# Conditioning rows one ahead, gate casts on VectorE, shorter conditioning stretches, and the modulated norm by pairs of blocks ahead of layer norms

## The chip, the cores and the metric

The kernel runs on one core of a Trainium2 chip. The metric is the device time of one execution in microseconds (us); below it stands as the median of three runs. All weights lie in HBM and are streamed once.

## What is computed

Two transformer nets in a row on 256 tokens of width 1024, two layers each, everything in float32. The first net has no conditioning; the second scales and shifts each normed input, and gates each branch, with vectors that are computed from one conditioning vector `c` (the six parts of `ada_w`). Cut to what matters here:

```python
for i in range(2):                                     # first net
    mix = concat(dsa_attention(...), spatial_gating(...)) @ w_o[i]
    x = layer_norm(ALPHA * x + mix, ln1_g[i], ln1_b[i])
    gate, up = split(x @ w_ffn_in[i], 2)
    x = layer_norm(ALPHA * x + (silu(gate) * up) @ w_ffn_out[i] + ple, ln2_g[i], ln2_b[i])

cond = silu(c)
for layer in range(2):                                 # second net
    sh1, sc1, g1, sh2, sc2, g2 = split(cond @ ada_w[layer] + ada_b[layer], 6)
    h = rms_norm(x, norm_mix[layer]) * (1 + sc1) + sh1
    x = x + g1 * (even_mixer(h) if layer == 0 else odd_mixer(h))
    h = rms_norm(x, norm_mlp[layer]) * (1 + sc2) + sh2
    a = relu(h @ mlp_w1[layer])
    x = x + g2 * ((a * a) @ mlp_w2[layer])
```

## The kernel before

**Products.** A float32 product is made as three products of parts: each weight unit (1024 columns of 128 rows, 512 KB) is split into a high part (`A.copy`, L417, on ScalarE) and the rest (`V.tensor_tensor` subtract, L418, on VectorE), each activation block likewise into `xh` and `xl`, and TensorE adds high by high, high by rest and rest by high (L446 to L448 for one half of the tokens; L467 to L469 and L482 to L484 where both halves are computed at once). The tokens are two halves of 128, `rr` = 0 and 1; their programs are generators that the main loop (from L1411 on) advances in turn, half 0 a little ahead.

**Order.** Weights come in one fixed order of units. `load` (L145) issues on SyncE's queue in program order into six buffers `w` (NW); the split goes into seven places `h`, `l` (NHI) and a few borrowed ones (`qTa`, `kTa`, `mix`). A list scheduler sets each engine's order; PRIORITY gives a group of instructions a head start in it, by so many places: `ln` 60 for layer norms, `mod` 15 for `modulated`, `ada` -15 for `conditioning`.

**Conditioning.** The generator `conditioning` (L663) goes through 12 jobs, first the shifts and scales of both layers, then the four gates. A job loads eight rows of `ada_w` (512 KB each, from the same six `w` buffers) and adds them up on VectorE (L673 for the first row, L675 for the other seven; in one buffer, `kTb`). A gate job then splits its sum as weights are split, the high part on ScalarE (L681), the rest on VectorE (L682), sums over the partitions with a matmul by ones (L686, L687) and adds the bias (L688). The main loop paces the steps of this generator: `conditioning_goal` spreads 45, 35 and 26 steps evenly over three stretches of units (`spans`, L1416): layer 0's feed-forward of the first net, layer 1's, and the first MLP of the second net, each up to where the next layer's input product begins. One more step comes after each of the last two stretches.

**Transitions.** `modulated` (L1040) makes the normed, scaled and shifted input of a mixer or MLP for one half. ScalarE squares x (L1047), GpSimd takes the power (L551), VectorE scales x by four blocks (L1053, into `hr`), TensorE transposes them (L1056). Then ScalarE applies scale and shift from PSUM, once for each of the four blocks into the high part `xh` and once again for each into `hid` in full float32 (L1061); VectorE subtracts `xh` from `hid` for all four together (L1063, 128x512), which gives `xl`. There are four such transitions: into the even mixer (about 640 to 653 us), into the first MLP (787 to 812), into the odd mixer (975 to 1002) and into the second MLP (1100 to 1130). Ahead of the first stands a layer norm (L560 to L568) of each half, ahead of the others the gated update of x (L1071, L1072). Just before the third the first MLP ends: its last hidden chunk goes through relu (L1029) and square (L1030) and is split by halves (L985, L986) before the last products, L446 to L448 on bank `a`. Into the odd mixer four tables of gains are also made (L292 to L295), from rows that are loaded into a `hid` buffer.

Of the kernel before, what the change touches and what calls it, by code (L numbers as in the profile page):

```python
# [14 lines left out]
AF = mybir.ActivationFunctionType  # L15
ALU = mybir.AluOpType
AX = mybir.AxisListType

P = 128
# [53 lines left out]

PRIORITY = {"mod": 15, "sb": 60, "sel": 30, "diff": 200, "ada": -15, "upd": 60, "fin": -15,
            "gelu": 400, "dil": 200, "rope": 400, "hd": -60, "sc": 60, "lat": -60, "ex": 30,
# [5 lines left out]
def body(ctx: ExitStack, tc: tile.TileContext, I, out):  # L81
# [51 lines left out]
    def r(ap):  # L133
        return ap.bitcast(F32R)
# [9 lines left out]
    def load(dst, src):  # L144
        ins = nc.sync.dma_start(dst, src)  # L145
        tc.keep_in_program_order(ins)
# [512 lines left out]

    COND_JOBS = [(l, j) for l in range(DEPTH) for j in (0, 1, 3, 4)] + [(0, 2), (0, 5), (1, 2), (1, 5)]  # L660
    COND_NAMES = ("sh1", "sc1", "g1", "sh2", "sc2", "g2")

    def conditioning():  # L663

        cond, ones, cols_a = C["cond"], C["ones"], C["cols_a"]
        for l, j in COND_JOBS:
            name = COND_NAMES[j]
            acc = new(act, [P, D], "kTb", 1)
            for k in range(KB):
                wt = new(ring, [P, UNIT], "w", NW)  # L670
                load(wt, I["ada_w_2"][l, k * P : (k + 1) * P, j * D : (j + 1) * D])
                if k == 0:
# [4 lines left out]
            if name[0] == "g":  # L677
                gt = new(act, [P, D], "par", 2)
                G.dma_start(gt, bcast(I["ada_b_2"][l : l + 1, j * D : (j + 1) * D], D))
                hi, lo = new(ring, [P, UNIT], "w", NW), new(ring, [P, UNIT], "w", NW)  # L680
                A.copy(r(hi), acc)  # L681
                V.tensor_tensor(r(lo), acc, hi, op=ALU.subtract)  # L682
# [357 lines left out]
    def modulated(l, rr, which):  # L1040
# [10 lines left out]
        for b0 in (0, 4):  # L1051
# [5 lines left out]
            full = new(act, [P, 512], f"hid{rr}", 2).rearrange("p (k n) -> p k n", k=4)  # L1057
            for dst in (r(hi[:, b0 : b0 + 4]), full):
                for j in range(4):
                    k = b0 + j  # L1060
                    A.activation(dst[:, j], ps[:, j * P : (j + 1) * P], AF.Identity, scale=sc[:, k : k + 1],  # L1061
                                 bias=sh[:, k : k + 1])
            V.tensor_tensor(r(lo[:, b0 : b0 + 4]), full, hi[:, b0 : b0 + 4], op=ALU.subtract)  # L1063
        return [(hi[:, k], lo[:, k]) for k in range(8)]
# [339 lines left out]
    def program(rr):  # L1404
        load_x(rr)
        for l in range(DEPTH):
# [8 lines left out]
    even, odd = first_unit["ein", 0], first_unit["oin", 0]  # L1415
    spans = [(first_unit["pg", 0, 0], first_unit["in", 1, 0]), (first_unit["pg", 1, 0], even),  # L1416
             (first_unit["w1", 0, 0], odd)]

# [86 lines left out]
```

## Time and profile before

| | |
|---|---|
| median of three runs | 1300.56 us (1298.23 to 1302.83) |
| the profiled execution | 1306.28 us |
| its span | 1304.6 us, that is 1.68 us lie outside the span |
| mean granted clock of TensorE | 0.991 |
| TensorE busy | 1269.1 us, 97% of the span |
| VectorE busy | 1030.9 us, 79% |
| ScalarE busy | 731.9 us, 56% |
| GpSimd busy | 47.1 us, 4% |
| the stretch 140 to 320 us (first feed-forward) | TensorE busy 180.00 of 180 us, DMA engines 87% |

The page is read from its shares to the stretches: TensorE's weight loads (PEld) run beside its matmuls, so the two shares do not add up. "idle before, releaser" in a row is how long the engine stood still ahead of an instruction and whose end let it go. The granted clock in a row by stretch is a share of full speed: 1.00 is 2.4 GHz, 0.50 is 1.2 GHz.

### The profile page before, as it was taken

To read this page: it belongs to the slowest core of one execution; us is meant where nothing else is said; L and a number is where in the kernel's file an instruction comes from. 1 tells how busy PE (TensorE), PEld (TensorE's weight loads), DVE (VectorE), ACT (ScalarE), POOL (GpSimd) and SP (SyncE) were. 2 spreads that over 40 slices of the span, in tenths; PEclk is the share of its full clock that TensorE was granted. 3 is DMA by queue.
4 is the path that set the end of the run, shared out by engine and by line. 5 is a ranking of instruction groups with operands and counts; after the bars stand their busy time and mean duration, and the time that the engine had idled before them with its cause. 6 is when DMAs were issued, how large, how long until landed. Compare 5 with 4: busy or idle time off the path is not lost.

```text
span 1304.6 us, 21751 instructions
## 1 busy us (share of the span) xinstructions
PE 1269.1 (97%) x7894; PEld 1130.3 (87%) x7894; DVE 1030.9 (79%) x2142; ACT 731.9 (56%) x1500; POOL 47.1 (4%) x109
## 2 busy tenths in 40 slices
PE   7999999999999999999899998999989999999998
PEld 6887999998888899999798986989877888799997
DVE  6979998987988999877779868776577997865552
ACT  5655445543565455444577767554447776854551
POOL 2010000000000000000110000000001000000000
PEclk9999999999999999999899999999989999999999
DMA  8545888995654689887454435776765635566631
GB/s 274 191 159 160 298 313 301 335 340 169 182 193 156 200 304 336 285 262 246 159 157 137 139 122 178 245 258 223 243 209 134 194 96 163 172 204 192 190 115 49
DMA packets 121804, 270.08 MB, mean 207 GB/s; under 512 B 9587, under 2 KB 30160, under 8 KB 121696
## 3 DMA queue, kind: packets, MB, share of 16 engines
q1 hardware_dynamic: 120304, 265.62, 62.2%
q0 software_dynamic: 1392, 3.07, 1.1%
q8 instruction: 62, 1.02, 0.3%
q14 instruction: 46, 0.38, 0.1%
HBM read 267.60 MB, written 1.05 MB: 206 GB/s over the span
## 4 chain that ended last, share of the span: by engine, by line
PE 80%; DVE 9%; DMA 4%; ACT 3%; issue 2%; POOL 1%; SPq 0%; POOLq 0%; DVEq 0%; ACTq 0%
PE m L469 10%; PE m L467 10%; PE m L468 10%; PE m L446 7%; PE m L448 7%; PE m L447 7%; PE a L482 5%; PE a L483 5%; PE a L484 5%; PE a L610 2%; DVE l L418 2%; PE a L446 2%; PE a L448 2%; PE a L447 2%; DMA w<-in_ada_w 1%
## 5 line engine op out<-in xcount | busy, mean ns | idle before, releaser
L417 ACT CAST h<-w 128x512 fp32r<-128x512 f32 (+3 forms) x634 | 354.2, 605 | 233.2 <-PE m L448 45.9
L418 DVE TENSOR_TENSOR l<-w,h 128x512 fp32r<-128x512 f32 (+3 forms) x634 | 399.5, 662 | 48.1 <-ACT h L417 47.2
L467 PE MATMUL m<-xh,h 128*128 128x256 f32 x832 | 232.5, 279 | 0.0
L468 PE MATMUL m<-xl,h 128*128 128x256 f32 x832 | 232.0, 279 | 0.0
L469 PE MATMUL m<-xh,l 128*128 128x256 f32 x832 | 232.0, 279 | 0.0
L446 PE MATMUL m<-h,xh 128*128 128x512 f32 (+3 forms) x544 | 208.2, 384 | 3.7 <-ACT h L417 3.0
L448 PE MATMUL m<-h,xl 128*128 128x512 f32 (+3 forms) x544 | 206.2, 381 | 4.4 <-DVE xl L1063 4.4
L447 PE MATMUL m<-l,xh 128*128 128x512 f32 (+3 forms) x544 | 206.0, 380 | 0.6 <-DVE l L418 0.4
L467 PEld LDWEIGHTS m<-xh,h 128*128 128x128 f32 x832 | 156.4, 188 | 0.4
L468 PEld LDWEIGHTS m<-xl,h 128*128 128x128 f32 x832 | 156.4, 188 | 0.3
L469 PEld LDWEIGHTS m<-xh,l 128*128 128x128 f32 x832 | 156.3, 188 | 0.2
L675 DVE SCALAR_TENSOR_TENSOR kTb<-w,cond,kTb 128x1024 f32<-128x1024 f32 x84 | 107.5, 1279 | 49.8 <-DMA w<-in_ada_w 49.3
L448 PEld LDWEIGHTS m<-h,xl 128*128 128x128 f32 x544 | 103.9, 191 | 18.2 <-DVE xl L1063 5.3
L446 PEld LDWEIGHTS m<-h,xh 128*128 128x128 f32 x544 | 104.2, 192 | 16.8 <-ACT h L417 3.8
L447 PEld LDWEIGHTS m<-l,xh 128*128 128x128 f32 x544 | 103.9, 191 | 13.8 <-DVE l L418 1.8
L482 PE MATMUL a<-h,hh 128*128 128x512 f32 x216 | 84.4, 391 | 0.0
L483 PE MATMUL a<-l,hh 128*128 128x512 f32 x216 | 84.4, 391 | 0.0
L484 PE MATMUL a<-h,hl 128*128 128x512 f32 x216 | 84.3, 390 | 0.0
L992 ACT CAST hh<-hid 128x512 fp32r<-128x512 f32 x44 | 27.3, 622 | 55.9 <-PE a L483 41.8
L417 ACT CAST qTa<-w 128x512 fp32r<-128x512 f32 x60 | 34.4, 622 | 34.0 <-DMA w<-in_w_ffn_in 12.8
L417 ACT CAST kTa<-w 128x512 fp32r<-128x512 f32 x60 | 34.8, 626 | 29.3 <-PE m L469 7.8
L484 PEld LDWEIGHTS a<-h,hl 128*128 128x128 f32 x216 | 40.7, 188 | 8.6
(455 smaller groups left out, 2469.9 us busy)
## 6 DMA issues: line engine op xcount, KB each, us to landing
w<-in_mlp_w SPq DMA_DIRECT2D x128, 512.0 KB, 4.3
w<-in_ada_w SPq DMA_DIRECT2D x96, 512.0 KB, 5.0
w<-in_w_ffn_in SPq DMA_DIRECT2D x80, 512.0 KB, 5.0
w<-in_w_ffn_out SPq DMA_DIRECT2D x44, 512.0 KB, 5.4
w<-in_odd_w_in SPq DMA_DIRECT2D x24, 512.0 KB, 4.4
w<-in_even_w_in SPq DMA_DIRECT2D x24, 384.0 KB, 3.6
w<-in_w_in SPq DMA_DIRECT2D x16, 512.0 KB, 5.5
w<-in_w_o SPq DMA_DIRECT2D x16, 512.0 KB, 5.7
```

Of the source, the lines that this page charges most:

```text
L417: split = [A.copy(r(ht[:, c]), wt[:, c]), V.tensor_tensor(r(lt[:, c]), wt[:, c], ht[:, c], op=ALU.subtract)]
L418: V.tensor_tensor(r(lt[:, c]), wt[:, c], ht[:, c], op=ALU.subtract)]
L446: T.matmul(ps, r(xh), r(wh[:, cols]), start=first, stop=False)
L447: T.matmul(ps, r(xh), r(wl[:, cols]), start=False, stop=False)
L448: mm = T.matmul(ps, r(xl), r(wh[:, cols]), start=False, stop=last)
L467: T.matmul(ps, r(wh[:, cols]), r(XH[:, :, k]), start=first, stop=False)
L468: T.matmul(ps, r(wh[:, cols]), r(XL[:, :, k]), start=False, stop=False)
L469: T.matmul(ps, r(wl[:, cols]), r(XH[:, :, k]), start=False, stop=last)
L482: T.matmul(ps, r(xh), r(wh[:, cols]), start=start and k == 0, stop=False)
L483: T.matmul(ps, r(xh), r(wl[:, cols]), start=False, stop=False)
L484: T.matmul(ps, r(xl), r(wh[:, cols]), start=False, stop=False)
L675: V.scalar_tensor_tensor(acc, wt, cond[:, k : k + 1], acc, op0=ALU.mult, op1=ALU.add)
```

## The change

Four things are changed.

1. `conditioning` issues the load of each `ada_w` row one step ahead of the step that adds it. It does not do so across two places (COND_PAUSES): the first row of jobs 5 and 9 is loaded in its own step.
2. The high part of a gate's sum is cast on VectorE (`V.tensor_copy`) instead of on ScalarE (`A.copy`).
3. The second and third stretch of conditioning begin later and end earlier: the second has 60 units instead of 74 for its 35 steps, the third 52 instead of 64 for its 26.
4. `modulated` has priority 100 instead of 15, and works by pairs of blocks: two activations into `hid`, a ScalarE cast of the pair into `xh` (128x256), a VectorE subtract of the pair into `xl`. The second set of activations is gone.

```diff
-PRIORITY = {"mod": 15, "sb": 60, "sel": 30, "diff": 200, "ada": -15, "upd": 60, "fin": -15,
+PRIORITY = {"mod": 100, "sb": 60, "sel": 30, "diff": 200, "ada": -15, "upd": 60, "fin": -15,
...
+    COND_PAUSES = (5, 9)
...
-        for l, j in COND_JOBS:
+        ahead = []
+
+        def fetch_row(job, k):
+            l, j = COND_JOBS[job]
+            ahead.append(new(ring, [P, UNIT], "w", NW))
+            load(ahead[-1], I["ada_w_2"][l, k * P : (k + 1) * P, j * D : (j + 1) * D])
+
+        for job, (l, j) in enumerate(COND_JOBS):
             name = COND_NAMES[j]
             acc = new(act, [P, D], "kTb", 1)
             for k in range(KB):
-                wt = new(ring, [P, UNIT], "w", NW)
-                load(wt, I["ada_w_2"][l, k * P : (k + 1) * P, j * D : (j + 1) * D])
+
+                if not ahead:
+                    fetch_row(job, k)
+                if k < KB - 1:
+                    fetch_row(job, k + 1)
+                elif job + 1 < len(COND_JOBS) and job + 1 not in COND_PAUSES:
+                    fetch_row(job + 1, 0)
+                wt = ahead.pop(0)
...
-                A.copy(r(hi), acc)
+                V.tensor_copy(r(hi), acc)
                 V.tensor_tensor(r(lo), acc, hi, op=ALU.subtract)
...
-            for dst in (r(hi[:, b0 : b0 + 4]), full):
-                for j in range(4):
+            for j0 in (0, 2):
+                pair, two = slice(b0 + j0, b0 + j0 + 2), full[:, j0 : j0 + 2]
+                for j in (j0, j0 + 1):
                     k = b0 + j
-                    A.activation(dst[:, j], ps[:, j * P : (j + 1) * P], AF.Identity, scale=sc[:, k : k + 1],
+                    A.activation(full[:, j], ps[:, j * P : (j + 1) * P], AF.Identity, scale=sc[:, k : k + 1],
                                  bias=sh[:, k : k + 1])
-            V.tensor_tensor(r(lo[:, b0 : b0 + 4]), full, hi[:, b0 : b0 + 4], op=ALU.subtract)
+                A.copy(r(hi[:, pair]), two)
+                V.tensor_tensor(r(lo[:, pair]), two, hi[:, pair], op=ALU.subtract)
...
-    spans = [(first_unit["pg", 0, 0], first_unit["in", 1, 0]), (first_unit["pg", 1, 0], even),
-             (first_unit["w1", 0, 0], odd)]
+    spans = [(first_unit["pg", 0, 0], first_unit["in", 1, 0]),
+             (first_unit["gate", 1, 0], first_unit["down", 1, 4]),
+             (first_unit["w1", 0, 1], first_unit["w2", 0, 6])]
```

Three places show how instructions move. The names are a buffer's tag and its running number; a digit before the first underscore, as in `hid0`, is the half. In the changed file the lines lie further down: L688 and L690 are the old L673 and L675, L1063 the old L1048, L1068 the old L1053, L1071 the old L1056, L1080 the old L1063.

VectorE at the transition into the even mixer, before: half 1's layer norm (L560 to L568) and half 0's first two `xl` (L1063).

```order
L560 BN_STATS ln_st_1235_7323<-x1_149 128x6
L418 TENSOR_TENSOR l_1259_7438<-w_1257_7436,h_1258_7437 128x336
L562 BN_AGGR ln_mv_1236_7326<-ln_st_1235_7323 128x2
L418 TENSOR_TENSOR l_1263_7466<-w_1261_7464,h_1262_7465 128x384
L563 TENSOR_SCALAR ln_mv_1236_7326<-ln_mv_1236_7326 128x1
L567 SCALAR_TENSOR_TENSOR x1_149<-x1_149,ln_mv_1236_7326,par_1186_7082 128x512 x2
L568 SCALAR_TENSOR_TENSOR x1_149<-x1_149,pw_y_1237_7329,par_1187_7084 128x512 x2
L1063 TENSOR_TENSOR xl_78<-hid0_1218_7238,xh_77 128x512
```

The same place after:

```order
L560 BN_STATS ln_st_1235_7321<-x1_149 128x6
L1080 TENSOR_TENSOR xl_78<-hid0_1218_7238,xh_77 128x256
L562 BN_AGGR ln_mv_1236_7324<-ln_st_1235_7321 128x2
L418 TENSOR_TENSOR l_1259_7434<-w_1257_7432,h_1258_7433 128x336
L1080 TENSOR_TENSOR xl_78<-hid0_1218_7238,xh_77 128x256
L563 TENSOR_SCALAR ln_mv_1236_7324<-ln_mv_1236_7324 128x1
L567 SCALAR_TENSOR_TENSOR x1_149<-x1_149,ln_mv_1236_7324,par_1189_7091 128x512
L1080 TENSOR_TENSOR xl_78<-hid0_1221_7254,xh_77 128x256
L568 SCALAR_TENSOR_TENSOR x1_149<-x1_149,pw_y_1237_7327,par_1190_7093 128x512
L1080 TENSOR_TENSOR xl_78<-hid0_1221_7254,xh_77 128x256
```

Half 0's `xl` moved from behind half 1's whole layer norm to between its first steps.

TensorE at the transition into the first MLP, before: half 0's transposes (L1056), its first products (bank `m0_1642`), and half 1's mixer output product (banks `m1_1673` and `m1_1678`, of which some rows are left out).

```order
L1056 MATMUL a0_1638_9088<-ident_70,hr0_1637_9086 128x128 x3
L446 MATMUL m0_1642_9105<-qTa0_1627_9045,xh_77 128x512
L447 MATMUL m0_1642_9105<-qTa1_1628_9046,xh_77 128x512
L1056 MATMUL a0_1638_9088<-ident_70,hr0_1637_9086 128x128
L446 MATMUL m1_1673_9230<-kTa_1585_8886,xh_77 128x512
L447 MATMUL m1_1673_9230<-kTa_1585_8886,xh_77 128x512
L448 MATMUL m1_1673_9230<-kTa_1585_8886,xl_78 128x512
...
L446 MATMUL m1_1678_9254<-h_1622_9027,xh_77 128x512
...
L448 MATMUL m0_1642_9105<-qTa0_1627_9045,xl_78 128x512
```

The same place after:

```order
L1071 MATMUL a0_1638_9083<-ident_70,hr0_1637_9081 128x128 x4
L446 MATMUL m0_1642_9099<-qTa0_1627_9041,xh_77 128x512
L447 MATMUL m0_1642_9099<-qTa1_1628_9042,xh_77 128x512
L448 MATMUL m0_1642_9099<-qTa0_1627_9041,xl_78 128x512
...
L446 MATMUL m0_1642_9099<-h_1644_9101,xh_77 128x512
...
L446 MATMUL m1_1673_9224<-kTa_1585_8882,xh_77 128x512
```

Before, twelve products of half 1 stand between half 0's first product and the first that reads `xl`; after, eighteen products of half 0 come in a row, three for each of six blocks, and half 1's follow.

ScalarE at the end of the first MLP, before: splits of the next weights (L417), the gate's cast (L681), relu (L1029) and the split by halves (L985).

```order
L417 CAST mix0_1958_11011<-w_1957_11010 128x512 x2
L681 CAST w_2005_11229<-kTb_1896_10649 128x1024
L417 CAST h_1963_11031<-w_1962_11030 128x512 x2
L417 CAST h_1966_11045<-w_1965_11044 128x512 x2
L1029 ACTIVATE hid0_1935_10917<-m0_1920_10784 128x512
L417 CAST h_1999_11194<-w_1998_11193 128x512
L1029 ACTIVATE hid1_1936_10920<-m1_1921_10785 128x512
L985 CAST hr0_1937_10923<-hid0_1935_10917 128x256
```

The same place after (L1044 is the old L1029, L1000 the old L985):

```order
L417 CAST mix0_1960_11009<-w_1959_11008 128x512 x2
L417 CAST h_1964_11026<-w_1963_11025 128x512 x2
L417 CAST h_1967_11040<-w_1966_11039 128x512 x2
L1044 ACTIVATE hid0_1939_10921<-m0_1924_10787 128x512
L417 CAST h_1999_11184<-w_1998_11183 128x512
L1044 ACTIVATE hid1_1940_10924<-m1_1925_10788 128x512
L1000 CAST hr0_1941_10927<-hid0_1939_10921 128x256
```

The gate's cast is gone from ScalarE's row; on VectorE it now stands 16 rows behind the last row sum (L690) of its job.

## Rows read from the trace of the kernel before

**Rows 1.** Section 1 of the page: busy time, share of the span and instructions.
```profile
PE 1269.1 (97%) x7894; PEld 1130.3 (87%) x7894; DVE 1030.9 (79%) x2142; ACT 731.9 (56%) x1500; POOL 47.1 (4%) x109
```

**Rows 2.** By stretch: length, then busy PE, PEld, DVE, ACT, POOL; PEclk, DMA share, GB/s.
```profile
140.00:320.00 180.00, 180.00 (x1310) 170.12 (x1309) 159.72 (x237) 84.89 (x154) 0.00 (x0) 1.00 0.87 301
460.00:600.00 140.00, 140.00 (x1066) 134.32 (x1065) 117.67 (x177) 69.62 (x125) 0.00 (x0) 1.00 0.88 302
786.00:812.00 26.00, 22.23 (x113) 17.38 (x112) 21.12 (x37) 20.64 (x54) 2.62 (x3) 0.93 0.62 198
1100.00:1130.00 30.00, 28.20 (x138) 21.65 (x138) 22.69 (x42) 23.12 (x57) 1.86 (x2) 1.00 0.38 122
...
643.80:650.30 6.50, 4.58 (x17) 4.43 (x18) 5.32 (x10) 3.18 (x11) 1.67 (x3) 0.50 0.91 324
970.40:974.70 4.30, 4.28 (x10) 3.04 (x11) 2.67 (x7) 1.47 (x4) 0.00 (x0) 0.50 0.80 236
999.00:1002.10 3.10, 2.91 (x11) 2.72 (x12) 3.10 (x7) 1.76 (x6) 0.00 (x0) 0.50 0.54 205
```

**Rows 3.** Timeline of PE behind three transitions: start, duration, instruction [idle before, releaser].
```profile
645.72 0.65 PE L448 MATMUL m<-h,xl 128*128 128x336 f32 x1 [4.44 <-DVE xl L1063]
...
970.42 0.80 PE L446 MATMUL a<-qTa,hr 128*128 128x512 f32 x1 [4.53 <-ACT hr L985]
...
999.19 1.97 PE L1056 MATMUL a<-ident,hr 128*128 128x128 f32 x8 [2.46 <-DVE hr L1053]
```

**Rows 4.** Timeline of ACT, half 0 into the even mixer.
```profile
639.54 1.50 ACT L1061 ACTIVATE xh<-a,mod0sh,mod0sc 128x128 fp32r<-128x128 f32 x4
640.93 1.51 ACT L1061 ACTIVATE hid<-a,mod0sh,mod0sc 128x128 f32<-128x128 f32 x4
```

**Rows 5.** Timeline of DVE, the same place.
```profile
640.71 0.69 DVE L560 BATCH_NORM_STATS2 ln_st<-x 128x6 f32<-128x512 f32 x1
...
642.33 1.40 DVE L567 SCALAR_TENSOR_TENSOR x<-x,ln_mv,par 128x512 f32<-128x512 f32 x2
643.65 1.41 DVE L568 SCALAR_TENSOR_TENSOR x<-x,pw_y,par 128x512 f32<-128x512 f32 x2
644.98 0.68 DVE L1063 TENSOR_TENSOR xl<-hid,xh 128x512 fp32r<-128x512 f32 x1
```

**Rows 6.** Timeline of ACT, end of the first MLP, then (last two rows) of the second.
```profile
964.46 1.05 ACT L681 CAST w<-kTb 128x1024 fp32r<-128x1024 f32 x1 [6.40 <-DVE kTb L675]
965.42 2.17 ACT L417 CAST h<-w 128x512 fp32r<-128x512 f32 x4
...
969.96 0.71 ACT L985 CAST hr<-hid 128x256 fp32r<-128x256 f32 x2 [0.88 <-DVE hid L1030]
...
1277.29 1.30 ACT L1029 ACTIVATE hid<-m 128x512 f32<-128x512 f32 x2 [6.67 <-PE m L469]
1278.65 1.42 ACT L985 CAST hr<-hid 128x256 fp32r<-128x256 f32 x4
```

**Rows 7.** Timeline of DVE into the first MLP (first row) and the odd mixer.
```profile
795.41 1.28 DVE L675 SCALAR_TENSOR_TENSOR kTb<-w,cond,kTb 128x1024 f32<-128x1024 f32 x1
...
996.84 0.22 DVE L292 TENSOR_TENSOR rope_ck<-turns,hid 128x64 f32<-128x64 f32 x1 [0.77 <-DMA hid<-in_moba_k_norm]
...
997.38 0.21 DVE L1048 TENSOR_SCALAR rms_s<-rms_s 128x1 f32<-128x1 f32 x1
```

**Rows 8.** Groups by line and shape: busy, mean ns of one, idle before and releasers.
```profile
L675 DVE SCALAR_TENSOR_TENSOR kTb<-w,cond,kTb 128x1024 f32<-128x1024 f32 x84 | 107.5, 1279 | 49.8 <-DMA w<-in_ada_w 49.3 <-DVE kTa L418 0.3
L673 DVE TENSOR_SCALAR kTb<-w,cond 128x1024 f32<-128x1024 f32 x12 | 9.0, 749 | 9.2 <-DMA w<-in_ada_w 9.2
...
L986 DVE TENSOR_TENSOR hr<-hid,hr 128x256 fp32r<-128x256 f32 x12 | 4.4, 418 | 0.0
```

**Rows 9.** Waits of SyncE's queue from 140 to 320: us in total, times, longest.
```profile
SPq L145 <- DVE l L418: 70.7, 44, 15.1
SPq L145 <- DVE kTb L675: 31.6, 26, 3.3
```

## The prediction

> **What bounds the kernel now.** I read the page's busy times first, then the time by stretch, then the waits. TensorE is busy for 1269.1 of the span's 1304.6 us [rows 1], so 35.5 us is all that can come back without less arithmetic. Nothing is to be had in the long feed-forward stretches: TensorE is busy 180.00 of 180 us and 140.00 of 140 there, at granted clock 1.00 [rows 2]. VectorE's 49.3 us of waiting for conditioning rows [rows 8] costs nothing by itself as long as TensorE has split weights in stock. What is lost stands at the start, at the end, and where one layer hands over to the next. At those places two things are paid: TensorE's idle time, and then the time in which its clock is granted at 0.50 (1.2 GHz) after the pause, in which busy time is worth half. I call the places T1 (into the even mixer), T2 (into the first MLP), T3 (end of the first MLP), T4 (into the odd mixer) and T5 (into the second MLP). At stake are:
> - T1: 4.44 idle [rows 3], and half of 4.58 busy at 0.50 [rows 2], 2.29: 6.7.
> - T2: 26.00 less 22.23 not busy, 3.8, and 0.07 of the clock over 22.23, 1.6 [rows 2]: 5.3.
> - T3: 4.53 idle [rows 3], and half of 4.28 [rows 2], 2.1: 6.6 (rounded down).
> - T4: 2.46 idle [rows 3], and half of 2.91 [rows 2], 1.5: 3.9.
> - T5: 30.00 less 28.20, 1.8, at full clock [rows 2].
>
> Together 24.3 us; the change touches all five places.
>
> **The change part by part. T3: the cast leaves ScalarE.** The chain here reads backwards. TensorE stands for 4.53 us until the last hidden chunk is split by halves (L985 on ScalarE) [rows 3]. Ahead of L985 on ScalarE stands relu, ahead of that four weight splits of 2.17 us together, and ahead of those the gate's cast L681, which began at 964.46 after 6.40 us in which ScalarE waited for VectorE's last conditioning row [rows 6]. ScalarE takes its instructions in order, so everything queued behind L681 stood with it. After the change the cast is on VectorE, behind the sum that it needs anyway, and the third stretch ends early enough that the last sum is made 16 VectorE instructions ahead of it. What is late next is then relu itself, behind TensorE's own product. The second MLP, which has no conditioning beside it, shows that form: relu waits for TensorE only, and L985 follows directly [rows 6]; TensorE has other products of the same bank to run meanwhile. So I take the whole 6.6; the lower bound is 5, if L985 still waits 0.88 for the square as it does now [rows 6] and TensorE pays that and some clock. Each of the four casts now takes VectorE between 0.75 (one fp32 source, 128x1024) and 1.28 (two sources) [rows 8], 3 to 5 us in all. That is covered: VectorE waits 49.3 us for conditioning rows [rows 8] that now land a step ahead. If this cover were gone, a cast would delay one weight split by about its own length.
>
> **T1: pairs ahead of the layer norm.** Half 0's `hid` is complete at 640.93 + 1.51 = 642.44 [rows 4], but its `xl` starts only at 644.98, behind half 1's layer norm, 1.40 and 1.41 [rows 5]. After the change the first `xl` stands behind L560 alone. ScalarE then needs two activations and a cast of 256 for a pair: 2 x 0.35 (1.39 between two groups of four [rows 4]) + 0.35 (half of 0.71 [rows 6]) = 1.05, so the first pair is ready at about 640.7. VectorE is in L560 from 640.71 for 0.69 [rows 5], then takes 0.42 for the subtract [rows 8]: TensorE starts at about 641.8 instead of 645.72, 3.9 us earlier, and with idle of half a microsecond left the clock's 2.3 should stay too. From this 6.2 I take off two things. TensorE needs six matmuls for a pair, at full clock 6 x 0.135 (half of 4.58 / 17 [rows 2]) = 0.8, while ScalarE delivers one in 1.05, over three further pairs 0.7 to 1: I take 0.9. And half 1's layer norm now waits behind four subtracts, 4 x 0.42 = 1.7 less the overlap with work that it has to wait for anyway: 1.0, which half 1's own products show unless half 0's cover it. That leaves 4.3; bounds 2.5 (nothing of the clock comes back, and half 1 pays half of the 1.0: 3.9 - 0.9 - 0.5) and 6.2.
>
> **T4: the odd mixer.** Half 1's L1053 waits for the mean square, L1048 at 997.38, which stands behind gain tables whose rows wait for DMA (0.77 at the last) [rows 7]. The order after still has these tables ahead of it. But they load into a `hid` buffer that half 0 gives back, and half 0 is done earlier by its new place. I take half of the 3.9, 2.0; bounds 0 and 3.9.
>
> **T2: the first MLP.** Before, twelve products of half 1 lie between half 0's first product and the first that reads `xl`; after, half 0's come in a row. So TensorE meets the wait for `xl` uncovered. On VectorE two weight splits and one conditioning row of 1.28 [rows 7] still stand between the scaling and the first subtract: 2 x 0.65 + 1.28 + 0.42 = 3.0, against the eight transposes (1.97 at half clock [rows 3], so 1.0) that TensorE runs meanwhile: about 2.0 to 2.2 idle here. Of the 3.8 not busy now no single row gives a split; I put a third, 1.2, at this point. Half 1's products later cover its own norm better than now. Net loss 1.0; bounds from 4 lost (the whole wait shown, and the clock with it) to 2 gained.
>
> **T5** has the same new order without conditioning rows in between: 0, from -1 to +1.
>
> **Stretches and rows ahead.** 35 steps in 60 units instead of 74 and 26 in 52 instead of 64 are no denser than the first stretch's 45 in 74, during which TensorE never stood [rows 2]. Their price is taken as nothing, with the second rival below as its bound.
>
> **More instructions.** 16 subtracts of 512 become 32 of 256, each pair 2 x 0.418 - 0.688 = 0.15 us dearer [rows 5, 8], 2.4 us of VectorE in all, on the path only at T1, where it is in the 0.42. ScalarE loses half of its activations and gains 16 casts; it becomes freer.
> The Trainium skill, VectorE: DVE Perf Modes, section on the TRN2 errata, speaks against this part: a fixed cost per instruction is paid again by every small tile, so tiles of 512 elements or more are to be preferred. By that rule the pairs would be a loss of 2.4 us and the sum 9.5 instead of 11.9; the rows agree on the price of a piece, and say that here a wait of 2.5 us is taken away with it.
>
> **The sum.** 6.6 + 4.3 + 2.0 - 1.0 + 0 = 11.9 us. The profiled execution is 1306.28, 5.7 above the median; its span of 1304.6 would become 1292.7. Against the median: 1300.56 - 11.9 = 1288.7.
>
> **The rivals.**
> - It doesn't do all that it says: conditioning rows still stand at T2, and what half 0 gains at T1 half 1 gives back. Then T3 6.6, T1 2.5, T2 -4, T4 0, T5 -1: 4.1 gained, 1296.5. For it speaks the order of VectorE at T2, against it that half 0's products cover half 1's norm.
> - The row ahead takes a `w` buffer. In the conditioning stretches one more of six buffers is held by a row that waits its turn. SyncE's queue waits there 70.7 + 31.6 = 102.3 us of 180 for a buffer [rows 9]; with five serving where six did, this grows by a fifth, 20.5, and by the same share 15.9 in the 140 us of the second stretch, 36.4 in all. The stock of split units takes a part: at most seven places of 180 / 74 = 2.4 us each, 17 per stretch. With half of it standing, 36.4 - 17 = 19.4 comes through: 1308.1. It decides as soon as TensorE's stock runs out in a stretch; against it is that TensorE shows not one pause there now, with DMA at 0.87 [rows 2].
> - Everything comes back: T1 6.2, T3 6.6, T4 3.9, T2 2: 18.7, 1281.9.
> - The pairs are dearer than the wait that they save (the 2.4 us all on the path): 1291.1.
>
> **How the numbers follow.** Chances: the forecast 0.57, dearer pairs 0.05, everything back 0.10, half done 0.20, the held buffer 0.08. A measurement of this kernel can tell 0.3%, 3.9 us, from no change: faster is below 1296.7, slower above 1304.5. The half-done case sits on that bound, so half of its 0.20 is "same": faster 0.57 + 0.05 + 0.10 + 0.10 = 0.82, same 0.10, slower 0.08. The range goes from 1282 (everything back) to 1299, the half-done case with the runs' own 2.3 above their median; left out are the held buffer, half of everything back and a little of the half-done case, 0.18.
>
> **What the changed profile would show.** T3: no pause over 1 us ahead of the products that read `hr`, and ScalarE's relu released by TensorE. T1: the first L448 near 641.8, the pause under 1 us, clock 1.00 behind it, and a new short pause ahead of half 1's products. T2: one pause of about 2 us ahead of the first L448 on `m0`, released by the pair's subtract. T4: the tables' DMA wait gone or shorter. VectorE's wait for conditioning rows well under 49 us. I am wrong if TensorE pauses in 140 to 320 or 460 to 600, or if the pauses at T1 and T3 merely move to half 1.

## The result, and the profile after

The changed kernel is slower: 1310.65 us median of six runs (1307.40 to 1312.00) against 1299.33 (1298.09 to 1302.83) of the kernel before; the ratio is 1.0077, 95% interval 1.0053 to 1.0100. The prediction was 1288.7, with a range of 1282 to 1299. The profiled execution took 1311.92 us, its span is 1310.2.

Section 1 of its page, beside [rows 1]:

```profile
PE 1267.7 (97%) x7894; PEld 1128.9 (86%) x7894; DVE 1035.5 (79%) x2162; ACT 718.8 (55%) x1464; POOL 46.6 (4%) x109
```

and the one row of its section 5 in which something new stands (busy, mean ns of one, idle before and its releaser):

```profile
L467 PE MATMUL m<-xh,h 128*128 128x256 f32 x832 | 233.1, 280 | 9.6 <-DVE mod1sc L718 9.5
```

TensorE has the same work and 97% again. But L467, the first product of a feed-forward unit, now waits 9.5 us, and for an addition of the conditioning. In the kernel before it never waited, as the same group of its instructions shows:

```profile
L467 PE MATMUL m<-xh,h 128*128 128x256 f32 x832 | 232.5, 279 | 0.0
```

The stretches of the changed kernel, in the columns of [rows 2], place it:

```profile
140.00:320.00 180.00, 179.85 (x1309) 169.94 (x1309) 160.34 (x238) 88.21 (x159) 0.00 (x0) 1.00 0.87 306
460.00:580.00 120.00, 120.00 (x895) 114.31 (x894) 105.59 (x153) 60.25 (x108) 0.00 (x0) 1.00 0.89 307
592.00:602.00 10.00, 1.40 (x6) 1.43 (x7) 7.05 (x14) 1.62 (x3) 0.00 (x0) 0.56 0.85 282
786.00:812.00 26.00, 21.65 (x125) 17.63 (x124) 17.63 (x39) 15.18 (x38) 1.47 (x1) 0.93 0.47 143
1100.00:1130.00 30.00, 29.78 (x157) 24.05 (x156) 24.52 (x48) 18.90 (x43) 0.55 (x1) 1.00 0.41 132
```

The feed-forward stretches are as full as before up to 580. Between 592 and 602 TensorE is busy 1.40 of 10 us. TensorE's timeline there, and at the transitions (start, duration, instruction, idle before and releaser):

```profile
589.20 0.31 PE L713 MATMUL m<-ada_q,quarters 128*128 128x32 f32 x2
...
590.83 0.28 PE L469 MATMUL m<-xh,l 128*128 128x256 f32 x1
600.60 0.55 PE L467 MATMUL m<-xh,h 128*128 128x256 f32 x1 [9.50 <-DVE mod1sc L718]
...
653.71 0.42 PE L446 MATMUL m<-h,xh 128*128 128x336 f32 x1 [0.87 <-ACT xh L1079]
657.87 0.42 PE L448 MATMUL m<-h,xl 128*128 128x336 f32 x1 [0.34 <-DVE xl L1080]
...
691.17 0.62 PE L446 MATMUL m<-h,xh 128*128 128x384 f32 x2 [1.50 <-ACT h L417]
...
805.69 0.50 PE L446 MATMUL m<-qTa,xh 128*128 128x512 f32 x1 [0.89 <-ACT xh L1079]
807.73 0.50 PE L448 MATMUL m<-qTa,xl 128*128 128x512 f32 x1 [1.31 <-DVE xl L1080]
...
1004.63 0.55 PE L1071 MATMUL a<-ident,hr 128*128 128x128 f32 x3 [0.89 <-DVE hr L1068]
```

and VectorE's in the pause:

```profile
593.38 1.28 DVE L690 SCALAR_TENSOR_TENSOR kTb<-w,cond,kTb 128x1024 f32<-128x1024 f32 x1 [3.41 <-DMA w<-in_ada_w]
594.58 2.49 DVE L418 TENSOR_TENSOR l<-w,h 128x512 fp32r<-128x512 f32 x4
...
598.57 1.28 DVE L690 SCALAR_TENSOR_TENSOR kTb<-w,cond,kTb 128x1024 f32<-128x1024 f32 x1 [1.50 <-DMA w<-in_ada_w]
599.78 0.68 DVE L718 TENSOR_TENSOR mod1sc<-m,cols_a 32x8 f32<-32x8 f32 x4
```

Read together: a shift or scale job ends with a small matmul (L713) into one of the two `m` banks of half 0, at 589.20. The next feed-forward product needs that bank. It comes free when VectorE reads it (L718). But VectorE takes its instructions in order, and ahead of L718 stand rows of the next job (L690), and these wait for DMA, 3.41 and 1.50 us. So TensorE, with nothing amiss in its weights, stood until 600.60.

Two executions can be lined up by the share of TensorE's matmul columns done. Done so for the changed kernel (1311.92) against a second trace of the kernel before (1297.93, the first experiment below):

| stretch of the second trace, us | what lies there | forecast, us | measured, us |
|---|---|---|---|
| to 583 | start, both first layers | 0 | +0.8 |
| 583 to 608 | the new pause | 0 | +11.1 |
| 633 to 784 | T1 (to 660) and the even mixer | -4.3 | -4.8, then +2.3 |
| 784 to 834 | T2 | +1.0 | +5.0 |
| 960 to 985 | T3 | -6.6 | -0.2 |
| 985 to 1035 | T4 | -2.0 | +0.1 |
| 1035 to 1135 | T5 | 0 | -0.3 |
| sum | | -11.9 | +14.0 |

### The profile page after: what moved, and what is told of

Its sections match the earlier page's. It is cut to its first block, busy times and chain, and to the rows that moved or that the text cites. A ratio compares the mean times of both kernels' runs of the same rounds, so it can differ in the third digit from the quotient of the medians.

```text
span 1310.2 us, 21731 instructions
## 1 busy us (share of the span) xinstructions
PE 1267.7 (97%) x7894; PEld 1128.9 (86%) x7894; DVE 1035.5 (79%) x2162; ACT 718.8 (55%) x1464; POOL 46.6 (4%) x109
## 5 line engine op out<-in xcount | busy, mean ns | idle before, releaser
L417 ACT CAST h<-w 128x512 fp32r<-128x512 f32 (+3 forms) x634 | 354.9, 604 | 260.2 <-PE m L468 51.9
L467 PE MATMUL m<-xh,h 128*128 128x256 f32 x832 | 233.1, 280 | 9.6 <-DVE mod1sc L718 9.5
L446 PE MATMUL m<-h,xh 128*128 128x512 f32 (+3 forms) x544 | 208.6, 384 | 6.3 <-ACT h L417 3.7
L448 PE MATMUL m<-h,xl 128*128 128x512 f32 (+3 forms) x544 | 206.0, 381 | 0.6 <-DVE xl L1080 0.6
L467 PEld LDWEIGHTS m<-xh,h 128*128 128x128 f32 x832 | 157.1, 189 | 10.4 <-issue 10.0
L690 DVE SCALAR_TENSOR_TENSOR kTb<-w,cond,kTb 128x1024 f32<-128x1024 f32 x84 | 107.7, 1282 | 52.7 <-DMA w<-in_ada_w 52.6
L446 PEld LDWEIGHTS m<-h,xh 128*128 128x128 f32 x544 | 104.1, 192 | 20.7 <-ACT h L417 4.4
L448 PEld LDWEIGHTS m<-h,xl 128*128 128x128 f32 x544 | 104.0, 191 | 14.0 <-DVE xl L1080 1.1
L417 ACT CAST kTa<-w 128x512 fp32r<-128x512 f32 x60 | 34.5, 619 | 34.9 <-PE m L469 7.7
L417 ACT CAST qTa<-w 128x512 fp32r<-128x512 f32 x60 | 34.9, 623 | 28.8 <-PE a L484 9.4
L417 ACT CAST mix<-w 128x512 fp32r<-128x512 f32 x60 | 34.6, 620 | 25.0 <-PE m L468 10.5
```

The costliest lines, as they stand in the source:

```text
L417: split = [A.copy(r(ht[:, c]), wt[:, c]), V.tensor_tensor(r(lt[:, c]), wt[:, c], ht[:, c], op=ALU.subtract)]
L446: T.matmul(ps, r(xh), r(wh[:, cols]), start=first, stop=False)
L448: mm = T.matmul(ps, r(xl), r(wh[:, cols]), start=False, stop=last)
L467: T.matmul(ps, r(wh[:, cols]), r(XH[:, :, k]), start=first, stop=False)
L690: V.scalar_tensor_tensor(acc, wt, cond[:, k : k + 1], acc, op0=ALU.mult, op1=ALU.add)
```

## The experiments

The times are medians of ten or twelve runs, where nothing else is said, each beside the median of the kernel before that was measured with it. The ratio and its 95% interval in brackets are an estimate of their own and differ a little from the quotient of the two medians.

**Was the first trace a common one?** The kernel before, unchanged.

> The kernel before, unchanged, for a second trace. The prediction took its terms from one execution of 1306.28 us, 7 us above the median of 1299.3. If that execution was a common one with a slow start, the idle ahead of the four transitions is as before (4.4, 3.8, 4.5, 2.5 us). If it lost more at the transitions than most executions do, the pauses here are shorter by some 5 to 7 us in all, and the gains of the forecast were too large by as much.

It took 1297.93 us, a single run. T1 was as before (4.45 idle), T4 1.91. T3 was not. ScalarE and TensorE at the end of the first MLP in this second trace:

```profile
959.30 1.05 ACT L681 CAST w<-kTb 128x1024 fp32r<-128x1024 f32 x1 [6.70 <-DVE kTb L675]
...
964.80 0.71 ACT L985 CAST hr<-hid 128x256 fp32r<-128x256 f32 x2 [0.86 <-DVE hid L1030]
...
966.36 0.50 PE L448 MATMUL a<-qTa,hr 128*128 128x512 f32 x1 [0.37 <-DVE hr L986]
```

The chain is that of [rows 6], the same cast behind the same row with even more waiting, and 5.5 us from the cast to the split by halves in both. But VectorE added the last row 5.2 us earlier. Most of that comes from three of the rows before it, for which it waited 1.48, 3.58 and 2.97 us here and 2.76, 4.48 and 4.51 in the first trace. TensorE was at the place at the same time in both (965.9 and 966.0), so it paused 0.37 us instead of 4.53. The term of 6.6 is the price of one execution.

**Reading the bank earlier**, on the changed kernel.

```diff
+                with tc.high_priority(400):
+                    ps = bank("m", 0)
+                    T.matmul(ps[:, 0:32], C["quarters"], part, start=True, stop=True)
...
+                    for q in range(4):
+                        at_q = slice(32 * q, 32 * q + 32)
+                        V.tensor_tensor(m[at_q], ps[at_q, q:32:4], bcol[at_q], op=ALU.add)
```

> The changed kernel; only the last step of a shift or scale job (the matmul by quarters and the four bias additions that empty its bank) gets a head start of 400 places, so that VectorE reads the bank ahead of more of the next job's rows. Theory A (TensorE stood 9.5 us at 591 us because the bank of the up product was still held by this job, whose reader stood behind the next job's rows on VectorE): the pause goes, 1299 to 1301. Theory B (the row ahead starves the weights): the pause stays or only changes its name, 1308 to 1312.

1304.39 us against 1301.24 (ratio 1.0025, 1.0007 to 1.0044): neither forecast. The pause near 590 is gone, as the stretch shows (columns of [rows 2]):

```profile
580.00:610.00 30.00, 30.00 (x228) 28.73 (x227) 23.82 (x40) 14.17 (x25) 0.00 (x0) 1.00 0.86 293
```

But the earlier matmul has to wait for its own bank, and TensorE in order with it, 0.61 to 1.12 us in three places. One of them in TensorE's timeline:

```profile
494.91 0.41 PE L714 MATMUL m<-ada_q,quarters 128*128 128x32 f32 x2 [1.01 <-DVE hid L1028]
```

In this execution T2 also cost 7.6 us, with the clock at 0.50 for some 13 us.

**The old stretches**, on the changed kernel.

```diff
-             (first_unit["gate", 1, 0], first_unit["down", 1, 4]),
-             (first_unit["w1", 0, 1], first_unit["w2", 0, 6])]
+             (first_unit["pg", 1, 0], even),
+             (first_unit["w1", 0, 0], odd)]
```

> The changed kernel with the three conditioning stretches of before; rows ahead, casts and pairs stay. Theory A: the last job of the second stretch ends behind the up product again, with 80 products instead of 14 between its matmul and the next product that needs the bank; no pause near 591, but the conditioning is near the transitions again: 1298 to 1303. Theory B: the row ahead still takes a buffer, 1306 to 1311.

1300.11 against 1301.24 (0.9985, 0.9967 to 1.0003): theory A. No pause near 590.

**No rows ahead**, on the changed kernel.

```diff
-                if not ahead:
-                    fetch_row(job, k)
-                if k < KB - 1:
-                    fetch_row(job, k + 1)
-                elif job + 1 < len(COND_JOBS) and job + 1 not in COND_PAUSES:
-                    fetch_row(job + 1, 0)
+                fetch_row(job, k)
                 wt = ahead.pop(0)
```

> The changed kernel, but every conditioning row is loaded in the step that adds it, as before; stretches, casts and pairs stay. Theory A: the place of the job's end between gate and up product is the same, seven rows instead of eight stand ahead of the reader, so a pause of 4 to 10 us stays near 591: 1304 to 1311. Theory B: the pause goes with the held buffer, 1297 to 1300.

1305.04 against 1301.24 (1.0017, 1.0002 to 1.0032): theory A. The pause stays at its place, half as long in this execution (with the clock behind it 7.5 us are lost there instead of 11.1), and by the two ratios the kernel is 0.6% faster than the changed one. TensorE's timeline:

```profile
593.52 0.55 PE L467 MATMUL m<-xh,h 128*128 128x256 f32 x1 [4.81 <-DVE mod1sc L713]
```

**The casts alone**, on the kernel before.

```diff
-                A.copy(r(hi), acc)
+                V.tensor_copy(r(hi), acc)
```

> The kernel before, with the cast of the gates on VectorE and nothing else. In the second trace of the kernel before the pause at the end of the first MLP was 0.37 us instead of 4.53: the execution that the prediction read was one of those in which a late conditioning row holds ScalarE. Theory C (a pause that comes in some executions, taken away by this part alone): the slow end of the spread goes, the median falls by 1.5 to 3 us against the kernel before of the same call, and no pause over 1 us at that place. Rival (the late row holds something else as well, VectorE's splits for one): median within 1 us of the kernel before, the pause comes back under another releaser.

1302.32 against 1300.20 (1.0010, 0.9994 to 1.0027), runs from 1297.51 to 1305.98. Theory C fell: the pause at T3 was 0.37 in this trace, but the spread is as wide as that of the kernel before. It does not come from T3 alone; in this execution T2 and T4 ran partly at clock 0.50. Nor does the cast alone keep the pause at T3 away, as two runs below show (1.43 and 1.88).

**Pairs and priority alone**, on the kernel before: the edit of `modulated` as in the diff of the change, and

```diff
-PRIORITY = {"mod": 15, "sb": 60,
+PRIORITY = {"mod": 100, "sb": 60,
```

> The kernel before, with the modulated norm by pairs and its priority 100, nothing else: loads, casts and stretches as before. Theory: into the even mixer 4.8 us gained, of which 1.9 are lost again at 680 to 690 us where TensorE catches up with ScalarE's splits; into the first MLP 2.5 to 5 lost; nothing at the other two: within 2 us of the kernel before. The prediction as made: 4.3 and 2.0 gained, 1.0 lost, 5.3 us faster.

1301.81 against 1300.20 (1.0013, 0.9995 to 1.0032): as expected of the theory. Lined up with the second trace, 4.6 us are gained at T1, 1.1 lost by 784, 4.6 lost at T2.

**The first transition alone, by pairs**: on the kernel before, with the casts.

```diff
-PRIORITY = {"mod": 15, "sb": 60,
+PRIORITY = {"mod": 15, "mod0": 100, "sb": 60,
...
-    @ranked("mod")
     def modulated(l, rr, which):
+        with at("mod0" if l == 0 and which == 1 else "mod"):
+            return modulated_at(l, rr, which)
+
+    def modulated_at(l, rr, which):
...
+            if l == 0 and which == 1:
+                for j0 in (0, 2):
...
+            else:
+                for dst in (r(hi[:, b0 : b0 + 4]), full):
```

> The kernel before, with the casts of the gates on VectorE, and pairs with priority 100 at the transition into the even mixer alone; the other three transitions, the loads and the stretches as before. Theory: the two parts that gain, without the ones that lose: 2 (casts, mean over executions) + 2.9 (first transition) = 5 us faster, near 1296. Rival (what the first transition gains is given back in full by 690 us): as the casts alone, 1298 to 1300.

1295.89 against 1300.20 (0.9972, 0.9956 to 0.9988): faster, as the theory said.

**The same by four blocks**: as the run before, without

```diff
-            if l == 0 and which == 1:
-                for j0 in (0, 2):
...
-            else:
```

> As the run before it (casts on VectorE, priority 100 at the first transition alone), but by four blocks as in the kernel before: only the place in the order differs. The first xl then waits for the whole hid (642.44 in the first trace) and half of the layer norm, some 1.3 us later than by pairs, while the first high part is not delayed by the pair's cast (0.86 us in the traces of the pairs). Theory: within 1 us of the run by pairs; the gain at this place comes from the order, not from the pairs. Rival: the pairs carry it, and this run is 2 us or more slower.

1296.31 against 1300.20 (0.9967, 0.9953 to 0.9982): no difference from the pairs can be seen. The first `xl` is later, as TensorE shows, but the high part is not:

```profile
644.71 0.42 PE L448 MATMUL m<-h,xl 128*128 128x336 f32 x1 [2.63 <-DVE xl L1066]
```

Here it is 2.63 once; by pairs 0.87 and 0.33, and then, ahead of the weight at 680, 1.51 instead of 0.46.

In both runs the pause at T3 was there, 1.43 us by pairs and 1.88 here, though the cast stands on VectorE. The split by halves now waits for the square (L1030), which stands on VectorE behind the last row, the sum's cast and four weight splits. This is what the rival of the run with the casts alone said: the late row holds VectorE as well. ScalarE and TensorE in the run by four blocks:

```profile
964.90 0.71 ACT L985 CAST hr<-hid 128x256 fp32r<-128x256 f32 x2 [4.15 <-DVE hid L1030]
...
965.36 0.50 PE L446 MATMUL a<-qTa,hr 128*128 128x512 f32 x1 [1.88 <-ACT hr L985]
```

**The stretch six units earlier**, on the changed kernel: same length, same density.

```diff
-             (first_unit["gate", 1, 0], first_unit["down", 1, 4]),
+             (first_unit["gate", 1, 0] + -6, first_unit["down", 1, 4] + -6),
```

> The changed kernel with its second conditioning stretch moved six units earlier, as long and as dense as it is (35 steps in 60 units). The jobs then end elsewhere among the products: the last of the shifts and scales takes its bank ahead of a gate product instead of between a gate and its up product, and only the first job of the stretch ends between the two (32 products ahead of the up product, four rows ahead of its reader, in a place where VectorE did not yet wait for rows). Theory A (the place of the job's end decides): no pause near 590, 1298 to 1301. Rival (a denser stretch starves VectorE and TensorE wherever the jobs end): a pause of 5 us or more stays, 1306 to 1312.

1300.64 against 1299.94 (1.0010, 0.9994 to 1.0025): theory A; by the two ratios 0.7% faster than the changed kernel. The stretch from 580 to 610 (columns of [rows 2]):

```profile
580.00:610.00 30.00, 30.00 (x220) 28.38 (x219) 17.82 (x29) 14.05 (x25) 0.00 (x0) 1.00 0.71 240
```

**The stretch four units later.**

```diff
-             (first_unit["gate", 1, 0], first_unit["down", 1, 4]),
+             (first_unit["gate", 1, 0] + 4, first_unit["down", 1, 4] + 4),
```

> The changed kernel with its second conditioning stretch moved four units later, same density. Now the last job ends behind an up product, and the one ahead of it ends between a gate and its up product, eight products ahead of the latter, with seven rows ahead of its reader. Theory A: the pause near 590 goes and another of 4 to 12 us comes some 25 to 35 us earlier, ahead of an L467 and released by the additions of the second layer's shift (mod1sh): 1303 to 1312. Rival (density): a pause at the old place. If it is neither, 1298 to 1301, the count of products does not decide.

1305.96 (four runs) against 1299.94 (1.0060, 1.0038 to 1.0081): theory A. The pause moved to where the count of products put it, with the releaser that was named (TensorE's timeline):

```profile
559.78 0.55 PE L467 MATMUL m<-xh,h 128*128 128x256 f32 x1 [5.30 <-DVE mod1sh L718]
```

and the old place is full (the stretch from 580 to 610):

```profile
580.00:610.00 30.00, 30.00 (x228) 28.71 (x227) 19.76 (x28) 13.66 (x26) 0.00 (x0) 1.00 0.89 299
```

**Rows ahead alone**, on the kernel before: `fetch_row` and its calls as in the diff of the change.

> The kernel before with the conditioning rows loaded one ahead, nothing else. The held-buffer rival of the prediction asks for up to 36 us at full price, 17 at its middle. Theory: the buffers are not what limits the feed-forward stretches; TensorE stays busy there and the time is within 2 us of the kernel before, VectorE's waits for rows hardly shorter (52.6 against 49.3 us in the changed kernel). Rival: 3 us slower or more, with pauses of TensorE between 140 and 320 or 440 and 625.

1300.57 against 1299.94 (1.0007, 0.9993 to 1.0021). The feed-forward stretches (columns of [rows 2]):

```profile
140.00:320.00 180.00, 180.00 (x1310) 170.12 (x1310) 159.46 (x237) 86.77 (x156) 0.00 (x0) 1.00 0.85 301
460.00:600.00 140.00, 139.39 (x1059) 133.57 (x1058) 119.14 (x178) 70.86 (x126) 0.00 (x0) 1.00 0.88 300
```

and VectorE's row additions, beside the first of [rows 8]:

```profile
L689 DVE SCALAR_TENSOR_TENSOR kTb<-w,cond,kTb 128x1024 f32<-128x1024 f32 x84 | 107.6, 1281 | 44.9 <-DMA w<-in_ada_w 44.5
```

TensorE is full (0.61 us short in the second), so the buffer that a row holds costs next to nothing. VectorE waits 44.5 us instead of 49.3 [rows 8] for these rows, and 3.1 instead of 9.2 for the first rows of the jobs: together 47.6 against 58.5, and against 54.5 in the second trace. So a row ahead hides 7 to 11 us of VectorE's waiting, and the time shows no gain from it.

**The first transition alone, without the casts**: as the run by four blocks, with `A.copy(r(hi), acc)` in the gate jobs as before.

> The kernel before with one edit: priority 100 for the modulated norm of the first transition. Blocks by four, casts, loads and stretches as before. Theory: the casts gave nothing by themselves (0.1%), so this edit carries the whole gain of the two runs before: 1296 to 1297.5, 0.25 to 0.33% faster. Rival (the casts make the gain last, by keeping the pause at the end of the first MLP away): 1298.5 to 1300.

1297.67 against 1299.94 (0.9986, 0.9970 to 1.0003): between the two forecasts. Whether the casts add something is not settled.

**Priority 100 at all four transitions, by four blocks**, on the kernel before.

```diff
-PRIORITY = {"mod": 15, "sb": 60,
+PRIORITY = {"mod": 100, "sb": 60,
```

> The kernel before with priority 100 for the modulated norm at all four transitions, blocks by four. Its order of TensorE into the first MLP is that of the changed kernel (half 0's products in a row). Theory D (the loss into the first MLP comes from this order, which takes away half 1's products as cover): 2 to 5 us lost between 784 and 835 against the second trace of the kernel before, the 2 to 3 gained at the first transition are spent, 1299 to 1302. Theory E (it comes from the pairs, whose high part is ready later): no loss there, 1296 to 1298.

1305.81 against 1298.59 (1.0052, 1.0035 to 1.0068): theory D, and more than it asked for. TensorE's waits for `xl` into the two MLPs:

```profile
795.00 0.50 PE L448 MATMUL m<-qTa,xl 128*128 128x512 f32 x1 [2.44 <-DVE xl L1063]
...
813.41 0.50 PE L448 MATMUL m<-qTa,xl 128*128 128x512 f32 x1 [2.33 <-DVE xl L1063]
...
1127.64 0.50 PE L448 MATMUL m<-qTa,xl 128*128 128x512 f32 x1 [2.33 <-DVE xl L1063]
```

In the second trace of the kernel before none of these three waits reaches 0.3 us. Lined up with it, this run loses 7.2 us at T2 and 2.8 at T5. In the run by pairs with the same priority, TensorE's timeline at T2 reads:

```profile
791.92 0.50 PE L446 MATMUL m<-qTa,xh 128*128 128x512 f32 x1 [0.88 <-ACT xh L1064]
793.51 0.50 PE L448 MATMUL m<-qTa,xl 128*128 128x512 f32 x1 [0.86 <-DVE xl L1065]
...
810.91 0.50 PE L446 MATMUL m<-qTa,xh 128*128 128x512 f32 x1 [1.10 <-ACT xh L1064]
```

So the order opens the wait, and the pairs shorten it, at the price of a later high part.

**Pairs alone**, on the kernel before: the edit of `modulated` as in the diff of the change, `mod` stays at 15.

> The kernel before with the modulated norm by pairs and its old priority 15. Its order of TensorE into the first MLP is nearly that of the changed kernel as well (half 0's products in a row, after four of half 1's), and at the first transition the xl stay behind half 1's layer norm. Theory D: the first transition gains little (under 2), the first MLP loses 2 to 5: 1300 to 1304. Theory E: the same loss, with 0.9 us ahead of a first high part. The two differ only in the run before this one; this one tells whether pairs alone gain anything.

1300.53 against 1298.59 (1.0017, 0.9996 to 1.0038). Pairs alone gain nothing: 1.4 at T1, 1.7 lost at T2, against the second trace. In this execution the pause at T3 was there, 2.64 us.

**The change repaired**: on the changed kernel, blocks by four as before, and

```diff
-PRIORITY = {"mod": 100, "sb": 60,
+PRIORITY = {"mod": 15, "mod0": 100, "sb": 60,
...
+        with at("mod0" if l == 0 and which == 1 else "mod"):
+            return modulated_at(l, rr, which)
...
-             (first_unit["gate", 1, 0], first_unit["down", 1, 4]),
+             (first_unit["gate", 1, 0] + -6, first_unit["down", 1, 4] + -6),
```

> The changed kernel with three of its numbers put right: the second stretch six units earlier, priority 100 at the first transition alone and 15 at the others, blocks by four. Rows ahead, casts and the shorter stretches stay. Theory: neither the pause near 590 nor the loss into the first MLP, and the gain of the first transition: 1295 to 1298, as the run with casts and the first transition alone. Rival (rows ahead or the denser stretches cost something of their own): 1299 to 1302.

1295.80 against 1298.59 (0.9976, 0.9959 to 0.9992), runs from 1294.41 to 1297.98: as expected. The stretch near 590 and the transition into the first MLP in it (columns of [rows 2]):

```profile
580.00:610.00 30.00, 30.00 (x220) 28.34 (x219) 17.82 (x28) 14.18 (x25) 0.00 (x0) 1.00 0.71 239
786.00:835.00 49.00, 45.89 (x274) 39.21 (x275) 41.29 (x66) 35.57 (x81) 2.92 (x3) 1.00 0.67 217
```

the latter in the second trace of the kernel before:

```profile
786.00:835.00 49.00, 45.23 (x268) 38.21 (x267) 41.56 (x68) 36.35 (x84) 2.62 (x3) 1.00 0.70 228
```

and in the changed kernel, which begins the same work 9.4 us later, and where TensorE is busy 3 us less and at a lower clock:

```profile
795.40:844.40 49.00, 42.28 (x246) 35.06 (x245) 37.40 (x64) 30.49 (x70) 2.62 (x3) 0.97 0.65 203
```

It is the changed kernel without its two faults, by the two ratios 1.0% faster than that, and with the two runs at the first transition with casts the fastest form here; the three cannot be told apart.

## Why the prediction was wrong, step by step

**Stretches and rows ahead: the step that failed.** The prediction gave them a price of nothing, and the pause near 590 cost 11.1 us. The price was taken on the evidence that TensorE never stood in the first stretch, at the same density [rows 2]. Density was not what mattered. With 60 units instead of 74 the jobs end elsewhere among the products: the bank of the last shift-and-scale job came between a gate product and its up product, 14 products ahead of the latter in TensorE's order, where before 80 products stood between that matmul and the next one that needed a bank. And ahead of the bank's reader on VectorE stood eight rows instead of five. The two shifted runs settle it: the same density six units earlier has no pause, four units later has it at the job before. Without the row ahead, with seven rows ahead of the reader, it was shorter (4.81 against 9.50, one trace each) and the kernel 0.6% faster by the two ratios: the row ahead does not make the pause, but seems to lengthen it. All of this stood in the order of the changed kernel; the prediction looked at the transitions alone and did not follow the moved steps to their ends.

**The held-buffer rival** named 1308.1, close to the measured time, and was wrong in its mechanism: rows ahead alone show no cost clear of noise (1.0007, 0.9993 to 1.0021), and TensorE does not run out of weights.

**T3: 6.6 forecast, 0.2 measured against the second trace.** The chain was read rightly, and in the changed kernel no pause is left: relu waits for TensorE and the split follows it, as forecast from the second MLP (ScalarE's timeline of the changed kernel):

```profile
973.67 0.60 ACT L1044 ACTIVATE hid<-m 128x512 f32<-128x512 f32 x1 [1.03 <-PE m L469]
...
975.31 0.70 ACT L1000 CAST hr<-hid 128x256 fp32r<-128x256 f32 x2
```

But the term was read from an execution 5.7 us above the median, and taken off the median. Lined up with that execution, the changed kernel does gain 5.8 us at T3. The prediction noted the 5.7 us and did not ask which pause they were. Among the seven traces with the old cast it was 4.53 and 2.64 us in two and under 0.6 in the other five, so it is likely that most of the runs behind the median were without it (an inference from these few traces). Against its own time the forecast would have been 1306.28 - 11.9 = 1294.4. And the cast is not what takes the pause away by itself: with the cast moved and everything else at T3 as before it was 0.37, 1.43 and 1.88. The seven traces of the changed kernel and its variants are without it, with the old stretches and without rows ahead too; which of the parts does it is not separated.

**T1: 4.3 forecast, 4.8 measured, 2.3 given back.** TensorE's start (the first L448 at 654.58, which is 642.6 without the 12.0 us lost ahead of it, against 641.8), the clock at 1.00 and a pause under 1 us came as forecast (0.87 and 0.34). What the forecast lacked is that the time gained is partly spent some 35 us later, where ScalarE's splits for the next weights are the limit: 1.50 us ahead of the L446 at 691, 0.45 at the same place before, and some clock with it.

**T2: 1.0 lost forecast, 5.0 measured.** The wait was named and its sign was right; the size was off beyond its own bound of 4 in this execution. In six other traces with the same pairs and priority it was 2.2 to 7.6. The forecast counted one wait for `xl`. There are two halves, each with a wait for the high part (0.89 ahead of the first L446, since the pair's cast comes after two activations) and one for `xl` (1.31), and the clock falls to 0.50 for some 3 us behind them. Priority 100 alone takes 7.2 here.

**T4: 2.0 forecast, nothing measured against the second trace** (2.2 gained against the first); the wait there fell to 0.89, but it had been 1.91, without a loss of clock, in the second trace too, and products behind it wait for other things now. **T5**: nothing, as forecast.

**More instructions.** The prices held: a pair's subtract takes 421 ns, the cast on VectorE 692, a little under the lower bound of 0.75 (groups by line of the changed kernel, columns of [rows 8]):

```profile
L690 DVE SCALAR_TENSOR_TENSOR kTb<-w,cond,kTb 128x1024 f32<-128x1024 f32 x84 | 107.7, 1282 | 52.7 <-DMA w<-in_ada_w 52.6
L1080 DVE TENSOR_TENSOR xl<-hid,xh 128x256 fp32r<-128x256 f32 x32 | 13.1, 421 | 9.0 <-ACT xh L1079 9.0
...
L696 DVE CAST w<-kTb 128x1024 fp32r<-128x1024 f32 x4 | 2.8, 692 | 0.1
```

The 52.6 us in the first row contradict one more sentence of the prediction: that VectorE's wait for rows would be well under 49. It is 38.4 in the repaired kernel and 36.2 in the run without rows ahead, so the row ahead does not decide it. The rule for tiles of 512 or more (the Trainium skill, VectorE: DVE Perf Modes, section on the TRN2 errata) is borne out as to the price, 2 x 0.42 against 0.68 [rows 5]. At the first transition, pairs and four blocks came out alike (1295.89 and 1296.31), and the four subtracts there would be only 4 x 0.15 = 0.6 us dearer, too little to tell. Where the order leaves `xl` uncovered, pairs paid (ratio 1.0013 against 1.0052 with the same priority).

## What to carry to other kernels

When side work is paced differently, follow each of its steps to its end in the order: which bank or buffer it holds there, who needs that next, and what stands ahead of its reader on an engine that runs in order. A reader behind instructions that wait for DMA lends their wait to everyone who needs its bank. And a term read from one execution is taken off that execution's own time, or checked in a second trace, before it is taken off a median; a priority that helps where an engine idles is to be given there alone, not to every use of the same helper.

## What was not expected of the hardware

The same program's executions differ by up to 12 us (1296.02 to 1307.54 over 35 runs), and two traces show one place: VectorE's waits for three DMA rows were 0.9 to 1.5 us longer in one of them, its last row of the job came 5.2 us later, and TensorE paused 4.53 us there instead of 0.37. TensorE's granted clock adds to it: at T2 it stayed at 1.00 in the second trace of the kernel before, and was 0.50 for about 10 us (790 to 800) in the run with the casts alone, whose order there was that of the kernel before, with idle times alike. What decided between the two was not found.
